# SSD stage of a hybrid encoder step: x and B transposed by VectorE in 32 by 32 blocks and a trip through DRAM, instead of by TensorE

## The chip, the cores and the metric

The kernel runs on one NeuronCore of one Trainium2 chip. Its metric is the device time of one execution in microseconds. Before the change it takes 2657.95 us, the median of three runs (2656.24 to 2657.99). All data are float32; matrix products take their operands as float32r pairs (a high part and the rest), so that one product of the reference is three matmuls.

## The reference

One layer of a streaming encoder for two request groups: 256 new frames of one prompt stream and 16 new frames of each of 8 running streams, together 384 token columns. What matters here is branch B, a Mamba-2 state space scan (SSD) over 8 groups of 8 heads:

```python
xbc, new_conv = causal_conv(xbc, st_conv, p['conv_w'], p['conv_b'])     # silu(conv), width 4
xh = xbc[..., :D_INNER].reshape(b, L, SSD_GROUPS, HEADS_PER_GROUP, SSD_HEAD_DIM)
Bm = xbc[..., D_INNER:D_INNER + SSD_GROUPS * D_STATE].reshape(b, L, SSD_GROUPS, D_STATE)
Cm = xbc[..., D_INNER + SSD_GROUPS * D_STATE:].reshape(b, L, SSD_GROUPS, D_STATE)
...
def step(h, inp):
    xc, dtc, Bc, Cc = inp
    cum = jnp.cumsum(dtc * A, axis=1)
    ...
    cb = jnp.einsum('btgn,bsgn->btsg', Cc, Bc)
    xdt = xc * dtc[..., None]
    y = jnp.einsum('btsgr,bsgrp->btgrp', cb[..., None] * decay, xdt)
    y = y + jnp.einsum('btgn,bgrpn->btgrp', Cc, h) * jnp.exp(cum)[..., None]
    last = cum[:, -1]
    w_end = jnp.exp(last[:, None] - cum)
    h = h * jnp.exp(last)[..., None, None] + jnp.einsum('bsgn,bsgr,bsgrp->bgrpn', Bc, w_end, xdt)
    return h, y
```

Around it stand a pooling branch, two gates, the output projection and a squared-ReLU MLP; the change leaves all of these alone.

## The kernel before

**Stages.** The program runs, in order, the first projections and the pooling branch (to 419 us), the SSD stage (eight groups, to 1135 us), the second gate, the SSD projection and merge, the output projection, and the MLP. The change is in the SSD stage only.

**Projections.** `proj` computes one 128-column tile of a projection for all 384 tokens: 16 k-tiles, fed as two weight halves of 128x1024 (512 KB each). `take` fetches a half with a DMA on the SyncE queue (`wfetch`, L63), and splits it into a high part on ScalarE (L70) and the rest on VectorE (L71). Three buffers each for the raw half (`w`), the high part (`wh`) and the low part (`wl`) let the split of a half begin when TensorE has finished the half three before it. `half` then issues 24 matmuls (`mm3w`, L98 to L100): per k-tile high by high, high by low, low by high. With `chain[0]` set, TensorE's halves and the lumps described next stay in program order.

**A group of the SSD stage.** Ten projections run per group g: B, C, x0, x1, x2, then x3, and z0 to z3. Their weight halves are called w_x_0, w_x_1 and w_z_j_0, w_z_j_1 in the profile. After each of B, C and the four x a causal convolution follows: `conv_in` scales the PSUM result into a buffer (VectorE L572, ScalarE copies), `taps` computes four taps (ScalarE L586, VectorE L588) and a Silu (ScalarE L592). The result holds 128 channels on the partitions and 384 tokens in the free dimension: `D.BT`, `D.CT`, `D.xs[j]`.

**Lumps.** Twice a group TensorE does the small products of the scan in one go, a "lump". The first stands between x2 and x3 and starts pair 0 (x0, x1) of this group while it ends pair 1 of the previous group; the second stands after z3, starts pair 1 (x2, x3) and ends pair 0. A lump holds `t_pp` (L678), `t_trx` (L635: three 128x128 transpositions of each of two x tiles into PSUM), in the first lump also `t_cb` (L625) and `t_trB` (L619: three transpositions of B), then `t_yT` (L656), `t_Y` (L664), `t_yi` (L643) and the state products `t_su` (L783).

**Around a lump.** `xside` (VectorE) multiplies the transposed x, read from PSUM, by dt and by the end weights (L721), and splits the second product into `xhl` (ScalarE L735, VectorE L736); parts of xhl go to DRAM and come back rearranged (`x_scr`, `xst`, L739 and L743, ten DMAs on SyncE). `bside` splits the transposed B into `Bhl` (L691, L692) and sends a part the same way (`b_scr`, `bst`, L694 and L698, nine DMAs on SyncE). `eside` computes the decay matrices E on ScalarE (L753 to L764) and masks them on VectorE (L765); `dside` decays the states (L768); `final` and `finish` do the D skip, the gate and the group norm.

**Order.** Each engine and each DMA queue works through its instructions in the order in which the build puts them there; SyncE's queue is shared by the weight halves, x_scr, xst, b_scr, bst and cbc (the broadcast sums for E). A DMA whose semaphore wait is not yet met holds up all that stand behind it on that queue.

The transpositions before the change:

```python
for b in range(3):
    i = te.transpose(tr[:, b * P : b * P + P], S.D.xs[j][:, b * P : b * P + P], ident)
```

## Time and profile before

| What | Value |
|---|---|
| median of three runs | 2657.95 us |
| the profiled execution's own time | 2657.36 us |
| its span | 2655.6 us |
| granted TensorE clock, mean | 0.999 |
| SSD stage, first to last lump | 458.6 to 1170.5 us |
| one group, from lump to lump | 90 us |
| SyncE DMA queue, share of 16 engines | 43.1% |

How to read it: the span is the time between the first and the last instruction of the profiled execution; about 2 us of its own time lie outside. Engines are PE (TensorE matmuls), PEld (its weight loads), DVE (VectorE), ACT (ScalarE), POOL (GpSimd) and SPq (SyncE's DMA queue). L12 is line 12 of the kernel before. A row of the chain of waits or of the timeline begins with the start and the length in us; a row by tile has minimum, median and maximum in ns; a row by groups ends with total busy us, mean ns of one, and the idle time before. In the table of windows stand start and end, length, then busy us and count for PE, PEld, DVE, ACT and POOL, then the granted clock, the DMA share and GB/s.

### The profile page before, as it was taken

To read this page: it belongs to the slowest core of one execution; us is meant where nothing else is said; L and a number is where in the kernel's file an instruction comes from. 1 tells how busy PE (TensorE), PEld (TensorE's weight loads), DVE (VectorE), ACT (ScalarE), POOL (GpSimd) and SP (SyncE) were. 2 spreads that over 40 slices of the span, in tenths; PEclk is the share of its full clock that TensorE was granted. 3 is DMA by queue.
4 is the path that set the end of the run, shared out by engine and by line. 5 is a ranking of instruction groups with operands and counts; after the bars stand their busy time and mean duration, and the time that the engine had idled before them with its cause. 6 is when DMAs were issued, how large, how long until landed. Compare 5 with 4: busy or idle time off the path is not lost.

```text
span 2655.6 us, 38356 instructions
## 1 busy us (share of the span) xinstructions
PE 2645.0 (100%) x15269; PEld 2466.7 (93%) x15269; DVE 1503.8 (57%) x2044; ACT 1169.1 (44%) x1820; POOL 135.2 (5%) x166
## 2 busy tenths in 40 slices
PE   9999999999999999999999999999999999999998
PEld 9998889999999999988888889999999999989897
DVE  6585335788787879856343336434444444444446
ACT  6443325557575756545322235433333333323233
POOL 0000000011111111120000000000000000000000
PEclk9999999999999999999999999999999999999999
DMA  7444445656665666657444543433333333334443
GB/s 273 150 133 159 147 147 204 202 198 219 208 235 204 214 211 223 220 200 253 171 152 163 188 159 131 143 135 135 135 135 135 135 135 135 136 136 136 137 136 130
DMA packets 146163, 451.35 MB, mean 170 GB/s; under 512 B 17920, under 2 KB 45120, under 8 KB 140992
## 3 DMA queue, kind: packets, MB, share of 16 engines
q1 hardware_dynamic: 134400, 389.90, 43.1%
q0 software_dynamic: 11584, 59.00, 6.0%
q8 instruction: 120, 1.97, 0.3%
q14 instruction: 59, 0.48, 0.1%
HBM read 407.11 MB, written 41.72 MB: 169 GB/s over the span
## 4 chain that ended last, share of the span: by engine, by line
PE 98%; DVE 1%; ACT 0%; DMA 0%; issue 0%; DVEq 0%; ACTq 0%
PE pj_up L99 6%; PE pj_up L98 6%; PE pj_up L100 6%; PE wd L143 6%; PE wd L142 6%; PE wd L141 6%; PE pj_x L98 5%; PE pj_x L99 5%; PE pj_x L100 5%; PE pj_z L99 3%; PE pj_z L98 3%; PE pj_z L100 3%; PE pj_sp L141 3%; PE pj_sp L143 3%; PE pj_sp L142 3%; PE pj_gb L141 2%
## 5 line engine op out<-in xcount | busy, mean ns | idle before, releaser
L98 PE MATMUL pj_up<-x1h,wh_up 128*128 128x384 f32 (+1 forms) x1024 | 333.9, 326 | 0.0
L100 PE MATMUL pj_up<-x1h,wl_up 128*128 128x384 f32 (+1 forms) x1024 | 333.7, 326 | 0.0
L99 PE MATMUL pj_up<-x1l,wh_up 128*128 128x384 f32 (+1 forms) x1024 | 333.7, 326 | 0.0
L71 DVE TENSOR_TENSOR wl_wd<-w_wd,wh_wd 128x1024 fp32r<-128x1024 f32 x126 | 154.3, 1225 | 241.8 <-ACT wh_wd L70 241.8
L141 PE MATMUL wd<-wh_wd,hh 128*128 128x512 f32 x756 | 286.5, 379 | 0.0
L142 PE MATMUL wd<-wl_wd,hh 128*128 128x512 f32 x756 | 286.5, 379 | 0.0
L143 PE MATMUL wd<-wh_wd,hl 128*128 128x512 f32 x756 | 286.5, 379 | 0.0
L70 ACT ACTIVATE wh_wd<-w_wd 128x1024 fp32r<-128x1024 f32 x126 | 133.1, 1056 | 322.6 <-PE wd L143 262.2
L70 ACT ACTIVATE wh_up<-w_up 128x1024 fp32r<-128x1024 f32 x126 | 133.1, 1057 | 292.4 <-PE pj_up L99 232.3
L71 DVE TENSOR_TENSOR wl_up<-w_up,wh_up 128x1024 fp32r<-128x1024 f32 x126 | 154.3, 1225 | 181.4 <-ACT wh_up L70 181.2
L98 PE MATMUL pj_x<-xgh,wh_x 128*128 128x384 f32 x768 | 251.9, 328 | 0.0
L99 PE MATMUL pj_x<-xgl,wh_x 128*128 128x384 f32 x768 | 250.4, 326 | 0.0
L100 PE MATMUL pj_x<-xgh,wl_x 128*128 128x384 f32 x768 | 250.4, 326 | 0.0
L99 PEld LDWEIGHTS pj_up<-x1l,wh_up 128*128 128x128 f32 x1024 | 193.5, 189 | 0.2
L98 PEld LDWEIGHTS pj_up<-x1h,wh_up 128*128 128x128 f32 x1024 | 193.5, 189 | 0.2
L100 PEld LDWEIGHTS pj_up<-x1h,wl_up 128*128 128x128 f32 x1024 | 193.5, 189 | 0.0
L100 PE MATMUL pj_z<-xgh,wl_z 128*128 128x384 f32 x512 | 166.9, 326 | 0.0
L99 PE MATMUL pj_z<-xgl,wh_z 128*128 128x384 f32 x512 | 166.9, 326 | 0.0
L98 PE MATMUL pj_z<-xgh,wh_z 128*128 128x384 f32 x512 | 166.9, 326 | 0.0
L71 DVE TENSOR_TENSOR wl_sp<-w_sp,wh_sp 128x1024 fp32r<-128x1024 f32 x64 | 78.4, 1224 | 154.0 <-ACT wh_sp L70 154.0
L143 PEld LDWEIGHTS wd<-wh_wd,hl 128*128 128x128 f32 x756 | 142.9, 189 | 20.3
L141 PEld LDWEIGHTS wd<-wh_wd,hh 128*128 128x128 f32 x756 | 142.9, 189 | 20.1
(333 smaller groups left out, 5884.1 us busy)
## 6 DMA issues: line engine op xcount, KB each, us to landing
w_up<-w_up SPq DMA_DIRECT2D x128, 512.0 KB, 3.2
w_wd<-w_down SPq DMA_DIRECT2D x128, 512.0 KB, 3.2
w_x<-w_in SPq DMA_DIRECT2D x96, 512.0 KB, 3.4
w_z<-w_in SPq DMA_DIRECT2D x64, 512.0 KB, 3.4
w_sp<-w_ssd SPq DMA_DIRECT2D x64, 512.0 KB, 3.3
w_ga<-w_ga SPq DMA_DIRECT2D x32, 512.0 KB, 3.3
w_pp<-w_pp SPq DMA_DIRECT2D x32, 512.0 KB, 3.2
hs<-ssm POOLq DMA_DIRECT2D x16, 1024.0 KB, 6.9
```

Source lines behind the costliest of these rows:

```text
L70: cut[0] = s.activation(h, w, AF.Copy)
L71: cut[1] = v.tensor_tensor(l, w, h.bitcast(F32), ALU.subtract)
L98: te.matmul(out, wh, xh, start=first, stop=False, **how)
L99: te.matmul(out, wh, xl, start=False, stop=False, **how)
L100: return te.matmul(out, wl, xh, start=False, stop=last, **how)
L141: te.matmul(out, mh, vh, start=k == 0, stop=False)
L142: te.matmul(out, mh, vl, start=False, stop=False)
L143: last[0] = te.matmul(out, ml, vh, start=False, stop=k == nk - 1)
```

## The change

The transpositions of B and x leave TensorE: `t_trB` and `t_trx` are removed with their PSUM tiles. In their place, `turned` transposes each 32 by 32 block of a 128x384 tile within itself on VectorE (`xb`), writes it to a DRAM tile `t_scr` with four DMAs of 32 partitions each (in runs of 32 elements, so that the blocks land where the full transposition has them), and reads the tile back with one DMA as token by channel. These six instructions are not emitted where the tile is made, but in the next `proj`, after its first half (`due`). There are 40 such tiles (8 B, 32 x). All 200 DMAs are on SyncE. `xb` takes its buffer from the two that the conv taps use (`cacc`). The read for B lands in the low half of `Bhl`, which `bside` then splits in place; the reads for x land in `S.xT` (one buffer), which `xside` multiplies in place instead of writing `xdw`.

```diff
+    due = []
+
     def proj(units, rhs, name):
         o = bank[0](f"pj_{name}")[:, :T]
         for q, src in enumerate(units):
             half(o, q, take(src, f"{name}_{q}"), rhs)
+            while due:
+                due.pop()()
         return o
...
+    t_scr = [dram.tile([T, P], F32, name=f"t_scr{i}") for i in range(40)]
...
+        def turned(src, i, o):
+            def fn():
+                xb = pd.tile([P, T], F32, tag="cacc", name=f"xb{i}")
+                v.transpose(xb, src)
+                scr = t_scr[i]
+                for q in range(4):
+                    p32 = slice(q * 32, q * 32 + 32)
+                    sy.dma_start(
+                        scr[:, p32].rearrange("(j a) b -> a j b", a=32), xb[p32].rearrange("p (j b) -> p j b", b=32)
+                    )
+                sy.dma_start(o, scr.rearrange("(b t) n -> t b n", b=3))
+
+            due.append(fn)
+
+        def xturned(D, g, j):
+            S = D.p[j // 2]
+            if j % 2 == 0:
+                S.xT = pd.tile([P, 2, 3, P], F32, tag="xT", name=f"xT{S.nm}", bufs=1)
+            turned(D.xs[j], g * 4 + j, S.xT[:, j % 2])
...
-        def t_trB(D):
-            D.tr = sstile(f"trB{D.g}")
-            for b in range(3):
-                i = te.transpose(D.tr[:, b * P : b * P + P], D.BT[:, b * P : b * P + P], ident)
-            return i
...
-        def t_trx(S):
-            S.trs = []
-            for j in S.js:
-                tr = sstile(f"trx{S.g}_{j}")
-                for b in range(3):
-                    i = te.transpose(tr[:, b * P : b * P + P], S.D.xs[j][:, b * P : b * P + P], ident)
-                S.trs.append(tr[:, :T].rearrange("p (b h q) -> p b h q", b=3, h=2))
             return i
...
         def bside(D):
-            D.Bhl = pd.tile([P, 2, 3, P], F32R, tag="Bhl", name=f"Bhl{D.g}")
             bh, bl = (D.Bhl[:, a].rearrange("p b n -> p (b n)") for a in range(2))
-            s.activation(bh, D.tr[:, :T], AF.Copy)
-            v.tensor_tensor(bl, D.tr[:, :T], bh.bitcast(F32), ALU.subtract)
+            s.activation(bh, bl.bitcast(F32), AF.Copy)
+            v.tensor_tensor(bl, bl.bitcast(F32), bh.bitcast(F32), ALU.subtract)
...
-            S.xdw = pd.tile([P, 2, 3, P], F32, tag="xdw", name=f"xdw{S.nm}", bufs=1)
-            for q, tv in enumerate(S.trs):
-                for o, i in ((S.xdt, 3), (S.xdw, 6)):
+            for q in range(2):
+                tv = S.xT[:, q].rearrange("p b (h q) -> p b h q", h=2)
+                for o, i in ((S.xdt, 3), (S.xT, 6)):
...
-            s.activation(S.xhl[:, 0], S.xdw, AF.Copy)
-            v.tensor_tensor(S.xhl[:, 1], S.xdw, S.xhl[:, 0].bitcast(F32), ALU.subtract)
+            s.activation(S.xhl[:, 0], S.xT, AF.Copy)
+            v.tensor_tensor(S.xhl[:, 1], S.xT, S.xhl[:, 0].bitcast(F32), ALU.subtract)
...
             D.BT = conv(u0, 32 + g, "BT", 2)
+            D.Bhl = pd.tile([P, 2, 3, P], F32R, tag="Bhl", name=f"Bhl{g}")
+            turned(D.BT, 32 + g, D.Bhl[:, 1].bitcast(F32))
...
             D.xs.append(conv(u0 + 2, g * 4, "xs", 6))
+            xturned(D, g, 0)
...
             D.xs.append(conv(u0 + 3, g * 4 + 1, "xs", 6))
+            xturned(D, g, 1)
...
-            lump(lambda: t_trx(S))
             lump(lambda: t_cb(D))
-            lump(lambda: t_trB(D))
...
             D.xs.append(taps(b2, g * 4 + 2, "xs", 6))
+            xturned(D, g, 2)
             D.xs.append(conv(u0 + 5, g * 4 + 3, "xs", 6))
+            xturned(D, g, 3)
...
-            lump(lambda: t_trx(S1))
```

More of the change, by code (lines that the diff above doesn't have):

```diff
@@ L627, in t_cb @@
                 )
-            return i
-        def t_trx(S):
-            S.trs = []
-            for j in S.js:
-                tr = sstile(f"trx{S.g}_{j}")
-                for b in range(3):
-                    i = te.transpose(tr[:, b * P : b * P + P], S.D.xs[j][:, b * P : b * P + P], ident)
-                S.trs.append(tr[:, :T].rearrange("p (b h q) -> p b h q", b=3, h=2))
             return i
```

## The prediction

> **What bounds the kernel now.** I read the page first: busy shares, then the chain that ended last.

> ```profile
> span 2655.6 us, 38356 instructions
> ...
> PE 2645.0 (100%) x15269; PEld 2466.7 (93%) x15269; DVE 1503.8 (57%) x2044; ACT 1169.1 (44%) x1820; POOL 135.2 (5%) x166
> ...
> PE 98%; DVE 1%; ACT 0%; DMA 0%; issue 0%; DVEq 0%; ACTq 0%
> ```

> TensorE is busy for 2645.0 of 2655.6 us and carries 98% of the chain: a matmul that goes away is worth its full time, and any wait that reaches TensorE costs its full time. So the question is what the removed transpositions take on that chain, and whether their replacement makes TensorE wait. I take the third group (g=2) as the sample; the chain of waits in order of time shows its two lumps:

> ```profile
> 634.88 0.71 PE py L678 x6
> 635.59 0.66 PE trx L635 x6
> 636.25 0.88 PE cb L625 x6
> 637.13 0.33 PE trB L619 x3
> ...
> 681.38 0.65 PE trx L635 x6
> ```

> **The gain.** The views of the two tiles give the count:

> ```profile
> L635 PE MATMUL trx<-cst,xs x96: 270/272/276, 458.4 to 1131.8; 128*128 128x128 f32 x96
> L619 PE MATMUL trB<-cst,xs x24: 272/272/273, 459.9 to 1087.2; 128*128 128x128 f32 x24
> ```

> A single record says 0.27 us, but records overlap; on the chain six take 0.655 us, so one is worth 0.109 us. 120 x 0.109 = 13.1 us. That is all the change can win.

> **What replaces them, and where it is queued.** Per tile: one VectorE transposition, four writes to DRAM and one read back, all five DMAs on SyncE, the queue that also fetches every weight half. Forty tiles add 200 DMAs there. A projection of 16 k-tiles is fed in two halves, and three halves are held split (bufs=3). The timeline of SyncE's queue before the change, in the mid-group lump of g=2:

> ```profile
> 626.19 11.25 SPq L63 DMA_DIRECT2D w_z<-w_in  x4
> 638.97 0.53 SPq L694 DMA_DIRECT2D b_scr<-Bhl  x1
> ```

> The four are z0_0, z0_1, z1_0 and z1_1: all issued by 637.4, before the lump's own DMAs. In the built changed program SyncE's queue reads differently there, in groups 1 to 7 alike:

> ```
> t_scr<-xb of x2   x4
> t_scr<-xb of x3   x2
> xT<-t_scr of x2
> t_scr<-xb of x3   x2
> w_z_1_1<-w_in
> w_z_2_0<-w_in
> xT<-t_scr of x3
> w_z_2_1<-w_in
> ```

> The load of z1_1 now stands behind the first write of x3's block, and that write waits for VectorE's transposition of x3, which waits for ScalarE's Silu of x3. Queued behind it are z2_0 and z2_1 too; the ScalarE and VectorE splits of z1_1 wait for the load, and TensorE for them. When does x3 get there, and when is z1_1 wanted? The windows from the start of x3's projection to the start of z1_1 (us, then busy times and counts):

> ```profile
> 641.04:648.94 7.90, 7.90 (x50) 7.90 (x49) 7.90 (x13) 7.89 (x22) 2.14 (x3) 1.00 0.65 225
> 648.94:660.64 11.70, 11.70 (x74) 11.70 (x73) 10.82 (x13) 10.97 (x19) 2.52 (x2) 1.00 0.80 274
> ```

> A half is 24 matmuls in 3.9 us (a few neighbours are counted at the edges). z1_1 starts three halves, 11.7 us, after x3 ends; its two first matmuls need only the high part, 0.3 us more. So the low part is wanted 12.0 us after x3's end. Now ScalarE's timeline:

> ```profile
> 647.87 0.68 ACT L755 ACTIVATE E<-cbc,tok 128x128 f32<-128x128 f32 x2
> ...
> 654.05 0.64 ACT L586 ACTIVATE cacc<-cbuf,vec 128x384 f32<-128x384 f32 x1
> ...
> 655.54 0.62 ACT L764 ACTIVATE E<-E 128x512 f32<-128x512 f32 x1
> 656.07 0.51 ACT L184 ACTIVATE nh_g<-ssum 128x384 fp32r<-128x384 f32 x1
> 656.48 0.31 ACT L578 COPY cbuf<-cstate 128x24 f32<-128x24 f32 x2
> 656.81 1.28 ACT L592 ACT_TABLE_LOAD   x1
> 658.11 0.61 ACT L592 ACTIVATE xs<-cacc,vec 128x384 f32<-128x384 f32 x1
> ```

> x3's Silu ends at 658.72, 9.8 us after x3's projection. Before, nobody cared. In the changed order ScalarE does after x3's end: the rest of the splits of z0_0, z0_1, z1_0 (2.1 us, at the 1.05 of a split below), a table load 1.28, eight exponentials of the second head pair at 0.3 each (2.4), the conv copies and first tap 0.8, two wide exponentials 0.85, the norm split 0.45, a table load 1.28, the Silu 0.6: 9.8 us again. The prices of the rest:

> ```profile
> L63 SPq DMA_DIRECT2D w_z<-w_in x64: 327/328/679, 453.1 to 1112.1; - x64
> L70 ACT ACTIVATE wh_z<-w_z x64: 1036/1052/1069, 459.3 to 1118.9; 128x1024 fp32r<-128x1024 f32 x64
> L71 DVE TENSOR_TENSOR wl_z<-w_z,wh_z x64: 1206/1222/1226, 465.7 to 1120.0; 128x1024 fp32r<-128x1024 f32 x64
> ...
> DMA to landing us min/median/max: 3.1/3.4/8.5
> ```

> ```profile
> L698 SPq DMA_DIRECT2D bst<-b_scr x64: 325/426/2029, 465.7 to 1095.4; - x64
> ...
> DMA to landing us min/median/max: 1.7/1.9/4.2
> ```

> ```profile
> L721 DVE TENSOR_TENSOR xdt<-trx,tok 128x384 f32<-128x384 f32 x4 | 2.2, 548 | 0.0
> L174 DVE TENSOR_SCALAR ny_g<-ssum 128x384 int32<-128x384 int32 x1 | 0.4, 354 | 0.0
> ```

> The chain to z1_1, from x3's end: Silu done 9.8; the block transposition, an operation the trace does not have, between 0.35 (the cheapest VectorE row on 128x384) and 1.22 (a weight split), taken at 0.5 like the row of the same shape; five DMA issues ahead of the load, between 0.33 (a weight load) and 1.06 (twice b_scr's 0.53) each, taken at 0.5, near bst's 0.43 and b_scr's 0.53: 2.5; landing of z1_1 3.4; split high 1.05; split low 1.22. Sum 18.5. Wanted at 12.0: **TensorE waits 6.5 us a group.** With all low ends (0.35, 1.65, landing 3.1, Silu 0.3 earlier) 16.9, a wait of 4.9; with all high ends (1.22, 5.3, landing 4.4) 23.0, a wait of 11.0.

> A part of the 6.5 falls earlier. z0_0's load stands behind x1's trip and its splits behind the whole lump on VectorE (before, its split stood at 635.86, ahead of the lump's products):

> ```profile
> L792 DVE TENSOR_TENSOR hs<-hs,su 128x512 f32<-128x512 f32 x8 | 5.0, 678 | 0.0
> L807 DVE SCALAR_TENSOR_TENSOR xs<-xs,vec,Y 128x384 f32<-128x384 f32 x4 | 2.3, 603 | 0.0
> L815 DVE TENSOR_TENSOR zs<-zs,xs 128x384 f32<-128x384 f32 x4 | 2.1, 548 | 0.0
> L768 DVE TENSOR_TENSOR hs<-hs,decb 128x2048 f32<-128x2048 f32 x2 | 5.4, 2687 | 0.0
> ```

> From the lump's first Y on VectorE does half of these rows (2.5 + 1.15 + 1.05 + 2.7), x1's two products (1.0), a tap, the E mask, yis and the low part of xhl (about 3): 11.4 us from 3.4 after the lump's start, then the split 1.2: ready at 16.0. TensorE wants it at 5.3 (the shorter lump) + 7.8 + 0.3 = 13.4: 2 to 2.6 us late. This wait is inside the 6.5, because x3's chain does not hang on z0_0: z1_1 then only waits 4 more.

> The rest I cost at nothing. B's, x0's and x1's trips have cover: x1's Silu is done some 3 us before the lump, five issues, a landing of 2 and a read of 2 to 3 us end about 4 us into the lump, and VectorE reaches that product 7 us in; if the trip were 4 us longer, VectorE would stall there and z0_0 with it. VectorE's 40 transpositions add 20 us, but only the queue order matters. The products read SBUF instead of PSUM; I take the same time. The in-place products and the slot that xb shares with the conv taps are free 10 us before they are used again.

> Group 0 has no previous pair, so x3's Silu comes early; but there z0_0's split is 3.5 late behind the same lump, and z1_0's load stands behind x2's writes and eight xst loads: about 2 more, 5.6 together.

> **Sum.** Waits 7 x 6.5 + 5.6 = 51.1; transpositions -13.1; net +38.0 us. On the profiled execution, span 2655.6 of a run of 2657.36, that is 2693.6 and 2695.4; the median of the runs, 2657.95, stands 0.6 above that run. I forecast 2695.

> **A rule that would add to it.** The trace shows one long idle of TensorE, at the end: no matmul runs from 2647.2 on, the granted clock (third number from the right) is still full up to 2650.8 and half from 2651.0:

> ```profile
> 2647.20:2650.80 3.60, 0.00 (x0) 0.00 (x0) 3.28 (x8) 1.02 (x3) 0.00 (x0) 1.00 0.46 163
> 2651.00:2655.00 4.00, 0.00 (x0) 0.00 (x0) 1.30 (x2) 0.00 (x0) 0.00 (x0) 0.50 0.71 262
> ```

> [...] My second wait is some 4 us, broken by two matmuls after 3.4, so I count no drop. If the clock fell in each group, one half (3.9 us) would run at half speed: 8 x 3.9 = 31 us more.

> **Rivals.**
> 1. The cover holds: all weights arrive in time and only the 13.1 us show: 2645. It is decided where z1_1's load is issued: it must go out within 6.0 us of x3's end (12.0 less 3.4, 1.05, 1.22 and an issue). For it: no half in the trace is late now. Against it: the Silu alone ends at 9.8. Chance 0.09.
> 2. Only z0_0 is late: 8 x 2.2 = 18 less 13 is +5: 2663. It needs x3's Silu 4 us earlier than before, on a ScalarE that has the same work after x3. Chance 0.08.
> 3. The clock drops in the new waits: 2695 + 31 = 2726. Chance 0.14.
> 4. The trip is long: the writes land in 128-byte runs and the trace has no such DMA. x2's read waits for x2's writes, two places ahead of z1_1's load. Writes that take 12 us instead of 2 push that load 6 us: 8 x 6 = 48 more, 2743. Against it: bst's 512-byte rows land in 1.9. Chance 0.08. [...]

> **How the numbers follow.** The forecast has 0.61, with its own range 2682 to 2712 (the low ends give 8 x 4.9 - 13.1 = +26; upward half of the way to the high ends). The high ends, 8 x 11.0 - 13.1 = +75, give 2733. The range reaches from rival 2 (2662) past rival 3 to 2733 and leaves out rival 1 and rival 4. About 0.2% (5.3 us) is what a measurement here tells from no change. Faster: rival 1, 0.09. Within 0.2%: most of rival 2, 0.05. Slower: 0.86.

> **What would show it.** Right: TensorE idle before z0_0 and z1_1 in every group, ended by the low splits of z; the stage from the first to the last lump longer by some 38 us, all else unmoved; SyncE's load of z1_1 waiting for VectorE's transposition; no trx or trB on TensorE. Wrong: z1_1's load issued before x3's Silu, or x3's Silu well under 9 us after its projection; a transposition over 1.2 us, an issue over 1 us or a granted clock under 1.00 in the stage would make it slower still.

## The result, and the profile after

| | before | after |
|---|---|---|
| median | 2657.95 us (5 runs, 2656.24 to 2658.12) | 2724.33 us (5 runs, 2721.01 to 2728.31) |
| ratio to before | | 1.0246, 95% interval 1.0235 to 1.0257 |
| span of the profiled execution | 2655.6 us | 2719.2 us |
| granted TensorE clock, mean | 0.999 | 0.991 |
| one group, closing lump to closing lump | 90.0 us | 96.4 to 98.7 us |

The change makes the kernel 2.5% slower. The forecast was 2695 (2662 to 2733): right in its sign and inside its range, 29 us low. The page of after, busy time and chain that ended last:

```profile
span 2719.2 us, 38493 instructions
...
PE 2661.9 (98%) x15149; PEld 2473.8 (91%) x15149; DVE 1534.1 (56%) x2084; ACT 1170.5 (43%) x1820; POOL 109.6 (4%) x166
...
PE 73%; DVE 6%; issue 1%; DMA 1%; ACT 1%; SPq 1%; DVEq 0%; ACTq 0%
```

TensorE does 120 transpositions less, yet it carries 73% of the chain instead of 98%. Where, says the tile `yis`, which VectorE makes once a lump, from group 0's first lump to group 7's last; first of before, then of after:

```profile
L728 DVE TENSOR_TENSOR yis<-py,tok x16: 410/414/417, 463.4 to 1135.8; 128x256 f32<-128x256 f32 x16
```

```profile
L737 DVE TENSOR_TENSOR yis<-py,tok x16: 411/416/420, 464.2 to 1199.5; 128x256 f32<-128x256 f32 x16
```

672.4 us became 735.3: 62.9 of the 63.6 us lie in the SSD stage. TensorE's longest waits in after (total us, times, longest):

```profile
PE pj_z L98 <- ACT wh_z L70: 22.4, 9, 4.0
PE pj_z L100 <- DVE wl_z L71: 22.3, 16, 2.4
...
PE pj_x L98 <- DVE cbuf L577: 1.2, 1, 1.2
```

In the SSD stage all are for the weights of z, save the last one, in group 0. The sample group again (g=2; x3's projection ends at 664.9). SyncE's queue, then ScalarE, then VectorE, in the timeline of after:

```profile
673.87 2.88 SPq L610 DMA_DIRECT2D t_scr<-xb  x5
676.93 0.38 SPq L613 DMA_DIRECT2D xT<-t_scr  x1
677.36 1.00 SPq L610 DMA_DIRECT2D t_scr<-xb  x2
678.39 0.95 SPq L63 DMA_DIRECT2D w_z<-w_in  x2
```

```profile
674.68 0.61 ACT L597 ACTIVATE xs<-cacc,vec 128x384 f32<-128x384 f32 x1
...
682.55 1.06 ACT L70 ACTIVATE wh_z<-w_z 128x1024 fp32r<-128x1024 f32 x1 [7.14 <-DMA w_z<-w_in]
```

```profile
666.70 1.21 DVE L71 TENSOR_TENSOR wl_z<-w_z,wh_z 128x1024 fp32r<-128x1024 f32 x1
...
675.33 0.58 DVE L606 STREAM_TRANSPOSE xb<-xs 128x384 f32<-128x384 f32 x1 [0.65 <-ACT xs L597]
...
683.64 1.23 DVE L71 TENSOR_TENSOR wl_z<-w_z,wh_z 128x1024 fp32r<-128x1024 f32 x1 [2.97 <-ACT wh_z L70]
```

Read downward in time: Silu of x3 done at 675.3, its block transposition at 675.9, z1_1's load issued at 678.4 behind five DMAs of the trips, high part at 682.55, low part done at 684.9. That is 20.0 us after x3's end; TensorE wanted it at 12.0. Above it the low part of z0_0, at 666.7 to 667.9, 2.4 us after TensorE asked for it. Then the windows of the same stretch (the number before the last two is the granted clock):

```profile
664.79:668.20 3.41, 0.90 (x4) 0.53 (x4) 3.41 (x3) 3.38 (x5) 0.57 (x1) 1.00 0.83 225
668.22:671.62 3.40, 3.40 (x12) 3.40 (x12) 3.40 (x6) 2.74 (x10) 0.00 (x0) 0.50 0.96 331
681.85:685.27 3.42, 0.95 (x4) 0.65 (x5) 1.63 (x3) 2.11 (x2) 0.00 (x0) 1.00 1.02 383
```

The first row is the window with the first wait, the third the window with the second. After the first TensorE works for 3.4 us at half clock, 12 matmuls in the time of some 21 (below, a drop); the same follows the second.

### The profile page after: what moved, and what is told of

It is laid out like the page before. It is cut to its first block, busy times and chain, and to the rows that moved or that the text cites. A ratio compares the mean times of both kernels' runs of the same rounds, so it can differ in the third digit from the quotient of the medians.

```text
span 2719.2 us, 38493 instructions
## 1 busy us (share of the span) xinstructions
PE 2661.9 (98%) x15149; PEld 2473.8 (91%) x15149; DVE 1534.1 (56%) x2084; ACT 1170.5 (43%) x1820; POOL 109.6 (4%) x166
## 4 chain that ended last, share of the span: by engine, by line
PE 73%; DVE 6%; issue 1%; DMA 1%; ACT 1%; SPq 1%; DVEq 0%; ACTq 0%
PE pj_up L99 6%; PE pj_up L98 6%; PE pj_up L100 6%; PE wd L147 6%; PE wd L146 6%; PE wd L145 6%; PE pj_x L98 3%; PE pj_x L99 3%; PE pj_x L100 3%; PE pj_sp L146 3%; PE pj_sp L145 3%; PE pj_sp L147 3%; PE pj_z L100 2%; PE pj_z L98 2%; PE pj_z L99 2%; PE pj_gb L145 2%
## 5 line engine op out<-in xcount | busy, mean ns | idle before, releaser
L71 DVE TENSOR_TENSOR wl_wd<-w_wd,wh_wd 128x1024 fp32r<-128x1024 f32 x126 | 154.3, 1225 | 241.8 <-ACT wh_wd L70 241.8
L70 ACT ACTIVATE wh_wd<-w_wd 128x1024 fp32r<-128x1024 f32 x126 | 133.1, 1056 | 322.6 <-PE wd L147 262.1
L70 ACT ACTIVATE wh_up<-w_up 128x1024 fp32r<-128x1024 f32 x126 | 133.1, 1057 | 292.2 <-PE pj_up L99 232.3
L71 DVE TENSOR_TENSOR wl_up<-w_up,wh_up 128x1024 fp32r<-128x1024 f32 x126 | 154.3, 1224 | 181.2 <-ACT wh_up L70 180.9
L98 PE MATMUL pj_z<-xgh,wh_z 128*128 128x384 f32 x512 | 177.6, 347 | 23.3 <-ACT wh_z L70 22.4
L100 PE MATMUL pj_z<-xgh,wl_z 128*128 128x384 f32 x512 | 177.3, 346 | 22.3 <-DVE wl_z L71 22.3
L99 PE MATMUL pj_z<-xgl,wh_z 128*128 128x384 f32 x512 | 175.6, 343 | 0.0
L71 DVE TENSOR_TENSOR wl_sp<-w_sp,wh_sp 128x1024 fp32r<-128x1024 f32 x64 | 78.4, 1224 | 154.0 <-ACT wh_sp L70 154.0
```

Source lines behind the costliest of these rows:

```text
L70: cut[0] = s.activation(h, w, AF.Copy)
L71: cut[1] = v.tensor_tensor(l, w, h.bitcast(F32), ALU.subtract)
L98: te.matmul(out, wh, xh, start=first, stop=False, **how)
L99: te.matmul(out, wh, xl, start=False, stop=False, **how)
L100: return te.matmul(out, wl, xh, start=False, stop=last, **how)
```

## The experiments

Times of group 0 and of single groups are read in TensorE's timeline at the Y products of the closing lumps; in after, group 0 takes 9.2 us more than before and the seven others 684.5 us against 630.1. Each ratio is to runs of the kernel before that were timed along with the run (medians 2658.3 to 2659.5 us).

**1. The trips on GpSimd's queue.** All 200 DMAs of the trips leave SyncE.

```diff
-                    sy.dma_start(
+                    gp.dma_start(
                         scr[:, p32]...
-                sy.dma_start(o, scr.rearrange(...))
+                gp.dma_start(o, scr.rearrange(...))
```

> The changed kernel with all 200 DMAs of the trips issued on GpSimd's queue instead of SyncE's; nothing else. Theory (late weights: the trips hold up the weight loads of z0_0 and z1_1 on SyncE's queue, and all else is cover): the loads of z go out early again, TensorE has no wait in the SSD stage and no half-clock stretch, and only the 13.1 us of transpositions show: 2645, between 2640 and 2655. Rival (the traffic of the trips in 128-byte runs slows every weight load, or the block transpositions crowd VectorE): the same traffic and the same VectorE work are left, so most of the loss stays: 2690 to 2725.

Measured 2710.24, ratio 1.0195 (1.018 to 1.021): a miss for the theory, and in the rival's range. The weights of z0 and z1 do come early now, but the trip got longer, and VectorE shows it (the tile view of xb, then its timeline in g=2, where x3 ends at 668.7):

```profile
L610 POOL DMA_DIRECT2D t_scr<-xb x160: 616/617/652, 440.3 to 1164.6; - x160
...
DMA to landing us min/median/max: 2.0/3.9/7.2
```

```profile
679.17 0.56 DVE L606 STREAM_TRANSPOSE xb<-xs 128x384 f32<-128x384 f32 x1
683.89 0.56 DVE L730 TENSOR_TENSOR xdt<-xT,tok 128x384 f32<-128x384 f32 x1 [4.16 <-DMA xT<-t_scr]
684.48 0.56 DVE L730 TENSOR_TENSOR xT<-xT,tok 128x384 f32<-128x384 f32 x1
684.96 1.22 DVE L71 TENSOR_TENSOR wl_z<-w_z,wh_z 128x1024 fp32r<-128x1024 f32 x1
```

The block's product waits 4.2 us for the trip, and behind it in VectorE's queue stands the low split of z2_0. In the mid-group lumps of groups 2 to 7 VectorE waits in the same way for x0's and x1's trips, and TensorE's state products with it:

```profile
PE su L792 <- DVE cbm L723: 10.8, 6, 4.2
```

So there are two queues in which a weight can be held up by a trip; taking it out of one is not enough.

**2. x3's trip two projections later.** `xturned(D, g, 3)` moves from after x3 to before `zproj(2)`.

> The changed kernel with the trip of x3 alone emitted two projections later (in z2 instead of z0), still on SyncE. Theory: z1_1's load no longer stands behind x3's write, so its wait (2.4 and 0.7 us a group) and the half-clock stretch after it go; the wait before z0_0 (2.4 us in the profile, 2.9 against the need) and its half-clock stretch of 3.4 us, which costs 1.7, stay: 8 x 4.6 - 13.1 = +24, 2682, between 2670 and 2695. Rival (traffic or VectorE): nothing is removed but only moved, 2710 to 2725.

Measured 2691.9, ratio 1.0122 (1.0107 to 1.0137): inside the expectation, but the theory holds in part. z1_1's wait, 2.8 to 4.2 us in after, is 2.4 us in group 1, 0.7 to 1.0 us in groups 2 to 4 and gone from group 5 on; z0_0's 2.4 us stay in every group from 1 to 7. TensorE's waits, then SyncE's queue in g=2 (x3 ends at 663.6):

```profile
PE pj_z L100 <- DVE wl_z L71: 20.7, 13, 2.4
PE pj_z L98 <- ACT wh_z L70: 4.6, 3, 2.5
```

```profile
667.00 4.12 SPq L752 DMA_DIRECT2D xst<-x_scr  x6
671.22 3.38 SPq L610 DMA_DIRECT2D t_scr<-xb  x4
674.70 0.89 SPq L63 DMA_DIRECT2D w_z<-w_in  x2
```

z1_1's load, the first of the last row, now stands behind x2's four writes and goes out 11.1 us after x3's end instead of 13.5. Its low part comes 14.8 to 17.7 us after x3's end (groups 1 to 7; 19.5 to 20.5 in after), still later than the 12.0 wanted. In groups 1 to 4 that still sets the group's length; from group 5 on TensorE comes later still, for z0_0's wait and the half clock behind it (a granted clock of 0.50 from 1132.25 on in group 7). The two waits are two causes: what stands ahead of z1_1's load on SyncE, of which x3's trip is a part, and the lump ahead of z0_0's split.

**3. No trips.** VectorE transposes into the target, nothing goes through DRAM, and the blocks stay where they are.

```diff
-                xb = pd.tile([P, T], F32, tag="cacc", name=f"xb{i}")
+                xb = ... if i >= 32 else o.rearrange("p b n -> p (b n)")
                 v.transpose(xb, src)
-                scr = t_scr[i]
...
-            s.activation(bh, bl.bitcast(F32), AF.Copy)
+            s.activation(bh, D.BT, AF.Copy)
```

> The changed kernel without the trips: VectorE transposes the 32 by 32 blocks straight into the tile that the products read, and for B the split reads the untransposed tile; the blocks are left where they are, so the output is not the reference's. No DMA of a trip is left, VectorE does all 40 transpositions. Theory: 13.1 us less than before, 2645, between 2640 and 2650. Rival (VectorE crowded by 40 transpositions of 0.58 us): still well over 2658.

Measured 2650.78, ratio 0.9972 (0.9961 to 0.9982). Every group from 1 to 7 takes 88.4 us, 1.63 less than before: 15 transpositions at 0.109. Group 0 is 4.2 us longer than before (mean granted clock 0.998, against 0.999), mostly by one wait:

```profile
PE pj_x L98 <- DVE cbuf L576: 3.1, 1, 3.1
```

So the gain is as computed, and VectorE's 40 transpositions cost nothing in groups 1 to 7.

**4 and 5. What the half clock costs.** Filler matmuls (run 4) keep TensorE busy ahead of z0_0 and z1_1; their results are not used. In run 5 only in groups 1 to 7.

```diff
+    def fill(name, q):
+        n = {("0", 0): 15, ("1", 1): 24}.get((name[-1], q), 0) if name[0] == "z" else 0
+        if n:
+            wt = sstile(f"fill_{name}")[:, :T]
+            with behind(last[0]):
+                for _ in range(n):
+                    last[0] = te.matmul(wt, onesr, xg[0][0], start=True, stop=True)
```

> The changed kernel with matmuls put into the waits, whose result nobody reads: 15 ahead of z0_0 (2.4 us) and 24 ahead of z1_1 (3.9 us) in each group, so that TensorE is busy while it waits for the weights. If the half-clock stretches come from the idle and cost time, they go and the time falls by about 1.7 us for each stretch that follows z1_1 (five groups) and by some 2 to 3 us in group 0: 2712, between 2706 and 2718. Rival (the record of the clock is a mark only, or the matmuls after a wait are slow for another reason): 2724 or more, with the matmuls that do not fit into the waits on top.

Measured 2722.17, ratio 1.0239 (1.0223 to 1.0254): a miss by 4 us. The mean granted clock rises from 0.991 in after to 0.998, and yet little time is gone. Groups 1 to 7 fell from 684.5 to 679.4 us, but group 0, where the fillers stand in front of weights that wait for other things, rose by 6.2. Hence run 5:

> The changed kernel with the filler matmuls ahead of z0_0 and z1_1 in groups 1 to 7 only (their results are not used). My theory (z1_1 comes 20 us after x3's end whatever TensorE does before, so that only the half-clock window after z1_1 costs time, 1.7 to 2.0 us in five groups): seven periods sum to 679 instead of 684.5 us, group 0 as in the changed kernel: 2717 (2713 to 2721). Rival (every half-clock window costs its 1.7 us): eleven windows less in groups 1 to 7, 2705.

Measured 2716.13, ratio 1.0217 (1.0202 to 1.0232), the seven groups in 678.4 us, the mean granted clock 0.998. Group 0 took 4.8 us more than in after's profiled execution here too, without fillers; that execution was the fastest of its five and this one the slowest of its four, so group 0 alone decides nothing. Windows of run 5 in g=2, where x3 ends at 668.8: the one with the first wait, now filled, then the two that in after follow the waits at half clock:

```profile
668.77:672.17 3.40, 3.22 (x19) 2.93 (x18) 3.40 (x3) 3.37 (x5) 0.57 (x1) 1.00 0.89 226
672.19:675.59 3.40, 3.40 (x22) 3.40 (x22) 3.40 (x6) 2.75 (x10) 0.00 (x0) 1.00 0.96 329
689.25:692.66 3.41, 3.34 (x20) 3.34 (x21) 2.85 (x6) 1.59 (x2) 0.00 (x0) 1.00 0.87 287
```

z1_1's low part is ready 19.8 and 20.4 us after x3's end in the two runs (g=2), against 20.0 in after; in groups 1 to 6 it is ready at 19.6 to 20.7, against 19.5 to 20.2. So the drop behind z0_0 costs nothing, since TensorE only arrives later at a wait whose end x3 sets; the drop behind z1_1 costs time. It came in five groups, which take 97.6 to 98.7 us in after; the two without it take 96.4 and 96.7, and the groups with fillers 96.3 to 97.3, save the last (98.6 and 98.1), where z1_1's low part came only 21.9 and 21.4 us after x3's end.

**6. z0_0's split ahead of the lump.**

```diff
             b2 = conv_in(u0 + 4, g * 4 + 2)
+            while len(ready) < 3:
+                ready.append((queue[0][1], wload(*queue.pop(0))))
```

> The trips are all kept; only z0_0's load and split are emitted ahead of the mid-group lump, and in groups 1 to 7 the planned order then puts z1_1's load ahead of the trips of x2 and x3 too (in group 0 z1_1's load still stands behind x3's writes). My theory (the weight loads are late because of their places in SyncE's and VectorE's queues, not because the trips are there): both waits go in groups 1 to 7, a group takes about 88.4 us as without the trips, group 0 keeps its loss of 9 us: 2645 + 10 = 2655 (2650 to 2664), and the half-clock windows go with the waits. Rival (the load of 200 more DMAs or x3's chain itself holds the group up, wherever the weight loads stand): z1_1's low part still comes 20 us after x3's end, 2715 to 2724.

Measured 2746.49, ratio 1.0329 (1.0314 to 1.0345): outside both. z0_0, z0_1, z1_0 and z1_1 are all in time in groups 1 to 7, and TensorE waits for the next one, z2_0, instead, first for its high part and then for the low one:

```profile
PE pj_z L100 <- DVE wl_z L71: 51.6, 8, 8.8
PE pj_z L98 <- ACT wh_z L70: 23.0, 8, 5.8
```

**7. The same with x3's trip in z2.**

> As the run before, and x3's trip is emitted in z2 instead of in z0. My theory: groups 1 to 7 as in the run before (88.4 us), and in group 0 z1_1's load no longer stands behind x3's writes, so that one of its waits goes: 2651 (2647 to 2660). Rival (x3's trip is now late for the second lump, whose products read it): VectorE waits there for xT in every group, 1 to 3 us each, 2660 to 2680.

Measured 2713.93, ratio 1.021 (1.0193 to 1.0227): outside both. z2_0's low part is 6.0 us late in all seven groups. The high part is ready at 679.25 in g=2; VectorE's timeline says what it does then:

```profile
680.00 0.56 DVE L195 TENSOR_SCALAR ssum<-bc_g 128x384 f32<-128x384 f32 x1 [2.67 <-PE bc_g L193]
680.59 0.36 DVE L178 TENSOR_SCALAR ny_g<-ssum 128x384 int32<-128x384 int32 x1
...
684.54 0.56 DVE L180 TENSOR_TENSOR na_g<-ny_g 128x384 f32<-128x384 f32 x1
685.02 1.22 DVE L71 TENSOR_TENSOR wl_z<-w_z,wh_z 128x1024 fp32r<-128x1024 f32 x1
```

Nine of the ten steps of the previous group's norm, which hang on a TensorE result (`bc_g`) that comes only at the end of z1_1, stand ahead of the split. In the built programs of before and after the splits of z2_0 and z2_1 stand ahead of `ssum`; in this one behind it. The build plans the order of each engine anew for every kernel, and no plan had been asked to keep weights first. Group 0's wait for z1_1, which the theory had go, stays too (4.2 us): there its load now goes out behind x2's trip.

**8. x2's trip in z1 as well.**

> As the run before, and x2's trip is emitted in z1 instead of in x3, so that no weight load of z0 or z1 stands behind the trip of x2 or x3 in any group. My theory: 2648 to 2655, group 0's loss at most 5 us. Rival (group 0 waits for z1_0 behind x_scr and the eight xst loads, which are not moved here): as the run before within 2 us.

Measured 2680.62, ratio 1.0084 (1.0069 to 1.0099): outside both. Group 0 improves by 5.2 us against the run before (3.1 left of its loss), as the theory had it, but groups 1 to 7 take 90.6 to 95.1 us: one to three splits of z are 0.7 to 2.7 us late in each, those of z2 in groups 1, 3, 5 and 7, those of z1_1 and z3_1 (once z0_1 too) in 2, 4 and 6. Another order, another weight.

**9. The norm queued behind the splits.** Run 7 and one more edge, that is, one more constraint on the order that the build plans.

```diff
-        v.tensor_scalar(hm, o, -0.5 / n, -0.5 * EPS, ALU.mult, ALU.add)
...
-        return newton(y, a, hm)
+        with later() if after else nullcontext():
+            v.tensor_scalar(hm, o, -0.5 / n, -0.5 * EPS, ALU.mult, ALU.add)
+            return newton(y, a, hm)
```

> The earlier run with z0_0's split ahead of the lump and x3's trip in z2, and one more edge: the previous group's norm (ssum and the Newton steps on VectorE) is queued behind the newest weight split; no work is left out. My theory (that run lost 6.0 us a group because the planned order put ten steps of the norm ahead of the low split of z2_0 on VectorE): the 6.0 us go to 0.5, the half-clock windows go, a group takes 88.4 to 89.2 us, group 0 keeps its loss of some 8 us against before: 2658 (2653 to 2666). Rival (z2_0 was late for its load behind x2's trip, and the norm only filled the time): the wait stays at 4 us or more, 2695 to 2714.

Measured 2660.15, ratio 1.0007 (0.9998 to 1.0016): as expected, and 54 us less than run 7 by one edge. VectorE in g=2:

```profile
671.74 1.23 DVE L71 TENSOR_TENSOR wl_z<-w_z,wh_z 128x1024 fp32r<-128x1024 f32 x1 [1.47 <-ACT wh_z L70]
...
673.43 1.22 DVE L71 TENSOR_TENSOR wl_z<-w_z,wh_z 128x1024 fp32r<-128x1024 f32 x1
...
675.03 0.55 DVE L198 TENSOR_SCALAR ssum<-bc_g 128x384 f32<-128x384 f32 x1
```

The splits go first. Four of seven groups take 88.4 us, to 0.02 us what they take without any trip; the others 89.3 to 90.2. All 200 DMAs and 40 transpositions are still there. Group 0 still loses 9.1, and behind the last lump TensorE waits 1.2 us that it did not wait before.

**10. x2's trip in z1 in group 0 alone.**

```diff
-            xturned(D, g, 2)
+            if g:
+                xturned(D, g, 2)
...
+            if not g:
+                xturned(D, g, 2)
             zproj(1)
```

> As the run before, and in group 0 alone x2's trip is emitted in z1 instead of in x3, so that z1_1's load there no longer stands behind it; the queues of groups 1 to 7 are the same. My theory (group 0's loss is the same mechanism, z1_1's load behind a trip's writes): 4 to 5 us less than the run before, 2653 (2649 to 2659), about what the transpositions gain less 3 us in group 0. Rival (group 0 waits for the eight xst loads, not for the trip): within 1 us of the run before.

Measured 2657.46 (2654.21 to 2662.72, 11 runs), ratio 0.9996 (0.9987 to 1.0005). Group 0's loss falls from 9.1 to 3.9 us in the profiled execution (span 2652.4), which is the fastest of the 11; the median falls only by 2.7, and the intervals of runs 9 and 10 overlap, so the 4 to 5 us of the theory are shown in that one trace alone. There z1_1's load goes out 7.5 us after x3's end, against 11.5 in run 9, although the xst loads still stand ahead of it. The version is 67 us faster than the changed kernel and no different from the one before. What is left in group 0 is mainly 2.1 us at x3's start, where `cbuf` of x2 stands behind x1's transposition and a split; curing that was not tried.

## Why the prediction was right, and where it was not

**The gain, 13.1 us.** Right: 1.63 us a group without the trips.

**The place of z1_1's load in SyncE's queue.** Right, and the cause of the larger wait: run 2 moves only x3's trip, and z1_1's low part comes 1.8 to 5.4 us earlier; in runs 6, 7 and 9, where z1_1's load goes out ahead of both trips in groups 1 to 7, it is ready 7.6 to 8.4 us after x3's end and never late. The chain summed to 18.5 us and took 20.0: the Silu came 10.4 us after x3's end (predicted 9.8), the block transposition took 0.58 (0.5), the five issues 2.5 (2.5), z1_1's landing 4.1 (3.4), the high split with its start 1.1 (1.05), the low split 1.2 (1.22). The mis-sized terms are the Silu and the landing; z's weights land in 4.6 us at the median in after, 3.4 before. z1_1 is 8.0 us late, not 6.5.

**z0_0 2 to 2.6 us late behind the lump, inside the 6.5.** Right in size (2.4), and right that it does not add to z1_1's: in the filler runs z1_1's end hardly moves with what TensorE does before it. Rival 2, z0_0 alone, comes true only in groups 5 to 7 of run 2: there z0_0's 2.4 us and the half clock behind it are the loss; in groups 1 to 4 z1_1's load is still what is late.

**Rival 1, the cover holds,** needed z1_1's load within 6.0 us of x3's end; it went out 13.5 us after.

**B's, x0's and x1's trips and VectorE's 40 transpositions at nothing.** Right for groups 1 to 7 by run 3 and, with the trips, by the four groups of run 9 at 88.4 us. With the slower trip of run 1 VectorE does stall at the product, as the text said of a trip 4 us longer; but what waits with it is TensorE's `su`, not z0_0.

**"My second wait is some 4 us, broken by two matmuls after 3.4, so I count no drop."** This is the step that failed: it put the clock at nothing. That a broken wait brings no drop was the author's estimate; the rows of before show one long idle only, unbroken, with the clock at 1.00 for its first 3.6 us and at 0.50 after that. In after the clock fell after the first wait of 2.4 us already, in six of the seven groups (in g=2 with TensorE busy for 0.90 of the window's 3.41 us), and after the second in five. Rival 3 (2726) is near the measured time, but not for its reason: it charged 3.9 us in each of eight groups, which no run shows; a drop lasts 3.41 us in after, at a granted clock of 0.50, and costs half of that. What counts is 8.3 us in the five groups (684.5 less 7 times 96.6) and 3.4 in group 0 (6.8 us at half clock). Run 5 won 6.1 of the 8.3 back; z1_1's low part came 1.9 us later in it, added up over the seven groups. A granted clock under 1.00 in the stage was among the prediction's own signs of a greater loss.

**Group 0, net 4.0 us.** Too low: 9.2, of which the clock is 3.4; of the rest, 1.2 is the wait for `cbuf`, which no step had. z0_0 is 4.3 us late (3.5 predicted), and the wait of 2 for z1_0 is one of 1.0 for z1_1.

**The sum.** Of the 29 us missed, some 12 are the longer chain (1.5 to 1.7 in seven groups), 8.3 + 3.4 the clock, 1.8 the rest of group 0, and 3.3 the distance of the median from the profiled execution (2721.0). The measured 2724 lies above the 2682 to 2712 that the forecast gave its own sum. It is inside the stated range only because that reached past rival 3 to the high ends of the chain (the landing of 4.4 in them comes from no row; z1_1's took 4.1 in g=2). So the hit owes something to luck. By its low ends, +26, the inner range would begin at 2684.

**Rival 4, the long trip,** falls: no run shows the 12 us that it assumed; the writes in 128-byte runs land in 1.9 us at the median and 5.4 at most, 7.2 in run 1 (tile view of xb in after):

```profile
L606 DVE STREAM_TRANSPOSE xb<-xs x40: 561/578/579, 437.2 to 1163.6; 128x384 f32<-128x384 f32 x40
...
DMA to landing us min/median/max: 1.6/1.9/5.4
```

## What to carry to other kernels

An operation added off the critical engine was paid here in queue places (z1_1's load went out 13.5 us after x3's end in g=2, 11.1 with x3's trip moved): ask which load or split stands behind its first instruction in the order of each engine and each DMA queue, and when the engine that sets the pace wants it. Moving one instruction in a planned order moves others: after each move read the built order of all queues again, and pin what feeds the busiest engine (here one edge was worth 54 us). Where the removed work is 0.5% of the time and the new work needs a trip, an equal time is the best that these runs reached.

## What the runs showed of the hardware

```profile
975.39:978.80 3.41, 1.28 (x6) 0.98 (x7) 1.96 (x3) 2.35 (x3) 0.00 (x0) 1.00 0.98 373
978.82:982.20 3.38, 3.38 (x13) 3.38 (x12) 3.00 (x4) 1.22 (x2) 0.00 (x0) 0.50 0.77 252
780.85:784.27 3.42, 1.87 (x10) 1.58 (x11) 2.56 (x3) 2.41 (x3) 0.00 (x0) 1.00 1.01 371
784.29:787.70 3.41, 3.41 (x23) 3.41 (x22) 3.25 (x6) 2.01 (x2) 0.00 (x0) 1.00 0.85 279
1071.00:1074.40 3.40, 1.84 (x12) 1.54 (x10) 1.11 (x2) 0.24 (x1) 0.00 (x0) 1.00 0.88 256
1074.45:1077.80 3.35, 1.87 (x10) 1.58 (x11) 1.79 (x3) 1.95 (x3) 0.00 (x0) 1.00 0.83 297
```

In run 2 a window with 1.58 us of 3.40 is followed by a granted clock of 0.50, and one with 1.97 by 1.00. Such a window need not be idle: in groups 2 to 7 of after it holds the wait of 2.4 us for z0_0 (in group 6 all but 0.2 us of it), with TensorE busy for 0.89 to 1.23 us, and half clock follows; in group 1 the same wait falls across two windows, with 2.09 and 2.23 us, and none does. Of the windows that are themselves at half clock in after, the one with 2.85 us (from 473.66) is followed by another, those with 2.86 and more by full clock. At half clock a matmul starts every 0.32 us, at full clock every 0.163 (timeline of after, g=2).

**On GpSimd the trips were slower to start and to land.** The same four writes were issued at 0.62 us each from GpSimd against 0.47 on SyncE and landed in 3.9 us against 1.9 (medians of run 1 and of after). What else was under way when each was issued differs between the two, so the share of the queue itself is not shown.

**With the trips the weights landed later.** z's weights land in 4.6 us at the median in after and in 4.7 in run 4, 3.4 before. In four groups of run 9, where the loads go out early, TensorE loses nothing all the same: 88.4 us a group, as in run 3 without the trips.
